# Loading four sets of parameter rows at the start, on ScalarE's queue, in a DeltaNet and attention trunk

## The chip, the cores and the metric

The kernel runs on one core of a Trainium2 chip. The metric is the device time of one execution in microseconds. The median of three runs before the change is 1419.02 us (1417.68 to 1421.04). Less is better.

## The reference, cut to what matters

One sequence of 512 tokens of width 1024 goes through two layers. The first mixes tokens with a gated DeltaNet, the second with sliding-window attention; each ends with a gated MLP that holds a causal depthwise convolution of width 3. All of it is float32.

```
h = x
h = h + gated_deltanet(rmsnorm(h, a_norm_w), a_w_in, a_conv_w, a_a_log, a_dt_bias, a_out_norm_w, a_w_out)
h = h + conv_gated_mlp(rmsnorm(h, ffn_norm_w[0]), ffn_w_up[0], ffn_conv_w[0], ffn_conv_b[0], ffn_w_down[0])
k, v = shared_kv(h, kv_norm_w, w_kv)
h = h + sliding_window_sink_attention(rmsnorm(h, b_norm_w), k, v, b_w_q, b_sinks, b_w_o, bias, mask)
h = h + conv_gated_mlp(rmsnorm(h, ffn_norm_w[1]), ffn_w_up[1], ffn_conv_w[1], ffn_conv_b[1], ffn_w_down[1])
return rmsnorm(h, final_norm_w)
```

The parameters that the change moves are vectors: the taps of the DeltaNet's convolution (a_conv_w, 4 x 4096), those of the MLP's convolutions (ffn_conv_w, 2 x 3 x 5632), the DeltaNet's output norm (a_out_norm_w, 128) and the final norm (final_norm_w, 1024).

## The kernel before, in words

Activations are held with channels on the 128 partitions and the 512 tokens along the free dimension. In that layout a per-channel parameter is wanted as a column: one number for each partition. In memory the parameters are rows. The helper `columns` (lines 227 to 238) makes the one out of the other: it loads up to 128 rows of 128 numbers into a staging tile, one load for each part, turns the tile on TensorE (line 235) into a bank of PSUM, and has VectorE copy it (line 237) into a constant tile. Its arguments choose the queue of the loads (`q`, SP's if nothing is said), the staging buffers (`tag`) and the bank (`place`). PSUM is divided into tags of banks: "d" has 3, "g" 2, "s" 2 and "p" 1. The staging tag "acc" has two buffers, "f" three.

Matmuls run at float32 accuracy as three products of rounded halves (lines 162 to 164): for each weight tile ScalarE makes the high half (line 132, whi) and VectorE the low half (line 133, wlo); activations are split in the same way into xh and xl.

The start runs as follows. SP loads x in four tiles of 128 tokens (line 204) and the first weights (line 210). ScalarE's queue loads the norm rows and MLP biases, and `columns` turns them (norm_c, line 240). For each tile of x, ScalarE sums the squares (line 258) and takes a root (259), and VectorE scales the tile (261). TensorE turns the tiles in eight slabs (line 266), by turns into banks of "s" and "g"; ScalarE and VectorE split each slab while they scale it with a column of norm_c (lines 172 and 173). Then `columns` makes cw_c, the taps of the DeltaNet's convolution (line 273, loaded on SP's queue, bank "g"), which `conv_silu` (lines 275 to 282) reads. The first projection of keys follows, and the gates (lines 305 to 391): two narrow loads on ScalarE's queue (309 and 310), a chain on ScalarE and VectorE, four transposes (370) into a bank of "g", a copy of it by ScalarE (374) and exponentials of it (383 to 391).

Behind the gates stand the other columns: onw_c (17 rows in four loads, line 413) and fcw (128 rows for each of the two MLPs, line 424), all on SP's queue, staged in "f" and turned into banks of "g". The first reader of onw_c is the gating of the DeltaNet's output (line 723), that of fcw the first MLP.

The DeltaNet's heads come in four groups, whose jobs are given a priority by the list ORDER (lines 30 to 38): projections, products of the keys (line 433) and of the decays (464 and 465), the solving of small triangular systems, the scan. A planner at build time puts every engine's instructions in an order, by priority and by when it reckons their inputs to be there; a queue or an engine then runs its own list in that order. SP and ScalarE issue the loads. A load that reuses a completion counter waits for the load that had it before.

Of the kernel before, what the change touches and what calls it, by code (L numbers as in the profile page):

```python
# [17 lines left out]
P = 128  # L18
# [23 lines left out]
def kernel(  # L42
# [27 lines left out]
    V, S, G, PE, SP = nc.vector, nc.scalar, nc.gpsimd, nc.tensor, nc.sync  # L70
# [36 lines left out]
    def row(tag, dt=F32, n=T):  # L107
        return main.tile([P, n], dt, tag=tag, bufs=ROWS[tag], name=nm(tag))
# [4 lines left out]
    def bank(tag):  # L113
        return psum.tile([P, T], F32, tag=tag, bufs=BANKS[tag], name=nm(tag))

    def const(shape, dt=F32, s="c"):
        return cp.tile(list(shape), dt, name=nm(s))
# [109 lines left out]
    def columns(parts, n, s, q=SP, tag="acc", place="g"):  # L227
        st = row(tag, n=P)
        r = 0
        for ap in parts:  # L230
            k = ap.shape[0]
            q.dma_start(st[r : r + k, :], ap)
            r += k
        ps = bank(place)
        PE.transpose(ps[:, :n], st[:n, :], ident[:n, :n])
        t = const([P, n], s=s)
        V.tensor_copy(t[:], ps[:, :n])
        return t
# [11 lines left out]
        q=S,  # L250
    )
    NA, NFFN, NKV, NB, CB = 0, 8, 24, 32, 40


    for c in range(NC):
        junk = main.tile([P, D], F32, tag="nt", bufs=2, name=nm("junk"))
        r = const([P, 1], s="rx")
# [5 lines left out]
    for k in range(KD):  # L263
# [3 lines left out]
        h, l = row("xh", F32R), row("xl", F32R)  # L267
# [2 lines left out]
        xl.append(l)  # L270


    cw_c = columns([a_conv_w[0].rearrange("j (r c) -> (j r) c", c=P)], 128, "cwc")

    def conv_silu(ps, t, o):
        acc = row("acc")
# [99 lines left out]
    def hc(ap):  # L376
# [31 lines left out]
    od = dp.tile([4, P, NC, T], F32, name="od")  # L408
    zd = dp.tile([HV, P, T], F32, name="zd")
    yd = dp.tile([HV, P, T], F32, name="yd")  # L410

    fconv_rows = ffn_conv_w.rearrange("l j (r c) -> l (j r) c", c=P)
    onw_c = columns(
        [
            fconv_rows[0, 128:132, :],
            fconv_rows[1, 128:132, :],
            a_out_norm_w,
            final_norm_w.rearrange("(r c) -> r c", c=P),
        ],
        17,  # L420
        "onwc",
        tag="f",
    )
    fcw = [columns([fconv_rows[l, 0:128, :]], 128, "fcw", tag="f") for l in range(2)]

    def key_norms(g):
        pr = slice(2 * g, 2 * g + 2)
# [1017 lines left out]
```

## Time and profile before

| | |
|---|---|
| median of three runs | 1419.02 us |
| the profiled execution | 1418.66 us |
| its span, first to last instruction | 1416.8 us |
| TensorE busy | 1384.8 us |
| VectorE busy | 1109.1 us |
| ScalarE busy | 748.0 us |
| columns' transposes (line 235) start at | 8.46, 18.99, 42.90, 45.96 (two) us |

All times inside the execution are microseconds from the start of its span. PE is TensorE's matmul side, PEld its weight loads, DVE is VectorE, ACT ScalarE, POOL GpSimd, SP the engine that only issues loads; a "q" behind a name is the engine's queue, in which loads are issued and waited for. A row of a timeline has the start, the duration, engine and line, operation, tile written and tiles read, and in brackets how long the engine had been idle and what ended that.

### The profile page before, as it was taken

To read this page: it belongs to the slowest core of one execution; us is meant where nothing else is said; L and a number is where in the kernel's file an instruction comes from. 1 tells how busy PE (TensorE), PEld (TensorE's weight loads), DVE (VectorE), ACT (ScalarE), POOL (GpSimd) and SP (SyncE) were. 2 spreads that over 40 slices of the span, in tenths; PEclk is the share of its full clock that TensorE was granted. 3 is DMA by queue.
4 is the path that set the end of the run, shared out by engine and by line. 5 is a ranking of instruction groups with operands and counts; after the bars stand their busy time and mean duration, and the time that the engine had idled before them with its cause. 6 is when DMAs were issued, how large, how long until landed. Compare 5 with 4: busy or idle time off the path is not lost.

```text
span 1416.8 us, 21740 instructions
## 1 busy us (share of the span) xinstructions
PE 1384.8 (98%) x8362; PEld 1166.5 (82%) x8362; DVE 1109.1 (78%) x2072; ACT 748.0 (53%) x1470; POOL 15.7 (1%) x37
## 2 busy tenths in 40 slices
PE   7999999999999999999999999999999999999997
PEld 5787888878877888888988889778788888988897
DVE  4996886968856447879878889788658888878996
ACT  7764576656647325444335446567544444444543
POOL 1000000000100000000000000000000000000000
PEclk9999999999999999999999999999999999999999
DMA  5333254172465323221443223322132221432222
GB/s 160 90 104 115 80 174 124 60 230 84 143 221 157 119 86 115 90 90 46 134 149 119 75 73 108 109 76 76 60 112 86 93 90 59 137 107 86 95 75 75
DMA packets 162299, 151.80 MB, mean 107 GB/s; under 512 B 24148, under 2 KB 150677, under 8 KB 162197
## 3 DMA queue, kind: packets, MB, share of 16 engines
q1 hardware_dynamic: 159938, 150.22, 33.0%
q8 instruction: 66, 1.08, 0.3%
q10 hardware_dynamic: 2259, 0.20, 0.1%
q14 instruction: 36, 0.29, 0.1%
HBM read 133.60 MB, written 15.75 MB: 105 GB/s over the span
## 4 chain that ended last, share of the span: by engine, by line
PE 85%; DVE 7%; DMA 4%; ACT 2%; issue 1%; SPq 0%; DVEq 0%; ACTq 0%
PE d L162 20%; PE d L164 20%; PE d L163 20%; PE g L198 2%; DVE wlo L133 2%; PE d L1207 1%; PE d L1211 1%; PE d L1209 1%; PE d L1054 1%; PE d L1052 1%; PE d L1053 1%; PE s L1054 1%; PE p L1303 1%; PE s L659 1%; PE s L1052 1%
## 5 line engine op out<-in xcount | busy, mean ns | idle before, releaser
L162 PE MATMUL d<-xh,whi 128*128 128x512 f32 x1128 | 444.2, 394 | 0.2
L163 PE MATMUL d<-xl,whi 128*128 128x512 f32 x1128 | 444.0, 394 | 0.0
L164 PE MATMUL d<-xh,wlo 128*128 128x512 f32 x1128 | 442.1, 393 | 0.8 <-DVE wlo L133 0.5
L132 ACT CAST whi<-stage 128x1024 fp32r<-128x1024 f32 (+2 forms) x234 | 227.4, 976 | 249.7 <-PE d L163 170.3
L133 DVE TENSOR_TENSOR wlo<-stage,whi 128x1024 fp32r<-128x1024 f32 (+2 forms) x234 | 263.3, 1128 | 70.2 <-ACT whi L132 69.3
L164 PEld LDWEIGHTS d<-xh,wlo 128*128 128x128 f32 x1128 | 211.6, 188 | 45.5 <-DVE wlo L133 1.0
L162 PEld LDWEIGHTS d<-xh,whi 128*128 128x128 f32 x1128 | 211.7, 188 | 44.8 <-ACT xh L172 0.5
L163 PEld LDWEIGHTS d<-xl,whi 128*128 128x128 f32 x1128 | 211.7, 188 | 43.1 <-issue 0.5
L280 DVE SCALAR_TENSOR_TENSOR acc<-d,cwc,acc 128x511 f32<-128x511 f32 (+2 forms) x96 | 70.6, 738 | 8.7 <-ACT acc L277 7.8
L913 DVE TENSOR_TENSOR sz<-d,p6s 128x512 f32<-128x512 f32 x59 | 40.6, 688 | 43.4 <-PE d L164 41.2
L935 ACT ACTIVATE dt<-dt 128x512 f32<-128x512 f32 x44 | 27.8, 632 | 78.3 <-DVE dt L918 78.3
L918 DVE SCALAR_TENSOR_TENSOR dt<-sz,fcw,dt 128x511 f32<-128x511 f32 (+1 forms) x60 | 44.8, 747 | 1.8 <-ACT dt L916 0.9
L918 DVE SCALAR_TENSOR_TENSOR va<-sz,fcw,va 128x511 f32<-128x511 f32 (+1 forms) x58 | 43.3, 747 | 0.9
L561 DVE TENSOR_TENSOR sT<-sT,p6s 64x31 f32<-64x31 f32 (+15 forms) x124 | 40.9, 330 | 2.0
L555 DVE TENSOR_TENSOR p6s<-sN,sT 64x31 f32<-64x31 f32 (+15 forms) x124 | 40.7, 328 | 1.9
L1276 ACT ACTIVATE dt<-dt,sm 128x256 f32<-128x256 f32 (+1 forms) x64 | 30.1, 471 | 21.5 <-DVE sm L1259 21.5
L132 ACT CAST whi<-st 128x768 fp32r<-128x768 f32 (+1 forms) x30 | 23.7, 791 | 30.1 <-PE p L1053 5.8
L913 DVE TENSOR_TENSOR zl<-d,p6s 128x512 f32<-128x512 f32 x29 | 20.0, 688 | 17.8 <-PE d L164 17.8
L682 ACT ACTIVATE rq<-o 128x128 f32<-128x128 f32 x64 | 19.0, 301 | 25.0 <-DVE o L677 22.0
L937 DVE TENSOR_TENSOR va<-dt,va 128x512 f32<-128x512 f32 x44 | 30.4, 690 | 1.2
L133 DVE TENSOR_TENSOR wlo<-st,whi 128x768 fp32r<-128x768 f32 (+1 forms) x30 | 26.8, 899 | 2.2 <-ACT whi L132 2.2
L916 ACT ACTIVATE dt<-sz,normc,fcw 128x512 f32<-128x512 f32 x30 | 24.4, 815 | 6.5 <-DVE sz L913 6.2
(769 smaller groups left out, 2873.2 us busy)
## 6 DMA issues: line engine op xcount, KB each, us to landing
stage<-in_ffn_w_up_dram SPq DMA_DIRECT2D x44, 1024.0 KB, 4.7
stage<-in_a_w_in_dram SPq DMA_DIRECT2D x23, 1024.0 KB, 5.5
stage<-in_ffn_w_down_dram SPq DMA_DIRECT2D x16, 768.0 KB, 4.3
stage<-in_a_w_out_dram SPq DMA_DIRECT2D x8, 1024.0 KB, 5.1
st<-in_ffn_w_down_dram SPq DMA_DIRECT2D x8, 768.0 KB, 5.2
zd<-sz SPq DMA_DIRECT2D x16, 256.0 KB, 2.6
od<-o SPq DMA_DIRECT2D x16, 256.0 KB
stage<-in_b_w_q_dram SPq DMA_DIRECT2D x4, 1024.0 KB, 5.0
```

The costliest lines, as they stand in the source:

```text
L132: S.copy(hi[:, :kt, :m], src)
L133: V.tensor_tensor(lo[:, :kt, :m], src, hi[:, :kt, :m].bitcast(F32), op=ALU.subtract)
L162: PE.matmul(ps, hi[:, k, :m], xh[k], start=first and k == 0, stop=False)
L163: PE.matmul(ps, hi[:, k, :m], xl[k][:], start=False, stop=False)
L164: done.append(PE.matmul(ps, lo[:, k, :m], xh[k], start=False, stop=last and k == kt - 1))
L280: V.scalar_tensor_tensor(acc[:, d:], ps[:, : T - d], col, acc[:, d:], op0=ALU.mult, op1=ALU.add)
L555: V.tensor_tensor(tv, N[:, s, s + 1 : 32].unsqueeze(2).to_broadcast([64, n, m]), Tm[:, s : s + 1, 0:m].to_broadcast([64, n, m]), op=ALU.mult,)
L561: V.tensor_tensor(Tm[:, s + 1 : 32, 0:m], Tm[:, s + 1 : 32, 0:m], tv, op=ALU.subtract)
L913: V.tensor_tensor(u[:], ps[:], rs[:], op=ALU.mult)
L918: V.scalar_tensor_tensor(acc[:, d:], u[:, : T - d], tap(2 - d, t), acc[:, d:], op0=ALU.mult, op1=ALU.add)
L937: V.tensor_tensor(b[:], a[:], b[:], op=ALU.mult)
L1276: S.activation(ej, ej, AF.Exp, bias=ngm[:, i : i + 1], scale=-1.0, accum_out=den[:, i : i + 1])
```

## The change

The three calls of `columns` for cw_c, onw_c and fcw move up, right behind norm_c and ahead of the code that squares, scales and turns x. All their loads go to ScalarE's queue (`q=S`), and each of the four tiles gets a bank: cw_c one of "s", onw_c that of "p", the two of fcw one of "g" and one of "s". What is loaded and computed stays the same.

```
+    cw_c = columns([a_conv_w[0].rearrange("j (r c) -> (j r) c", c=P)], 128, "cwc", q=S, place="s")
+    fconv_rows = ffn_conv_w.rearrange("l j (r c) -> l (j r) c", c=P)
+    onw_c = columns(
+        [
+            fconv_rows[0, 128:132, :],
+            fconv_rows[1, 128:132, :],
+            a_out_norm_w,
+            final_norm_w.rearrange("(r c) -> r c", c=P),
+        ],
+        17,
+        "onwc",
+        q=S,
+        tag="f",
+        place="p",
+    )
+    fcw = [columns([fconv_rows[l, 0:128, :]], 128, "fcw", q=S, tag="f", place="gs"[l]) for l in range(2)]
...
-    cw_c = columns([a_conv_w[0].rearrange("j (r c) -> (j r) c", c=P)], 128, "cwc")
...
-    fconv_rows = ffn_conv_w.rearrange("l j (r c) -> l (j r) c", c=P)
-    onw_c = columns(
...
-        17,
-        "onwc",
-        tag="f",
-    )
-    fcw = [columns([fconv_rows[l, 0:128, :]], 128, "fcw", tag="f") for l in range(2)]
```

More of the change, by code (lines that the diff above doesn't have):

```diff
@@ L410 @@
     yd = dp.tile([HV, P, T], F32, name="yd")
-    fconv_rows = ffn_conv_w.rearrange("l j (r c) -> l (j r) c", c=P)
-    onw_c = columns(
[L414 to L419, printed above, removed]
-        17,
-        "onwc",
-        tag="f",
-    )
-    fcw = [columns([fconv_rows[l, 0:128, :]], 128, "fcw", tag="f") for l in range(2)]
     def key_norms(g):
```

## The prediction

> **What bounds the kernel now.** I read the page first, then the two ends of the stretch that the change touches: TensorE's timeline from 40 us, the waits of the load queues, and the timelines of the first 15 us.
>
> ```profile
> span 1416.8 us, 21740 instructions
> PE 1384.8 (98%) x8362; PEld 1166.5 (82%) x8362; DVE 1109.1 (78%) x2072; ACT 748.0 (53%) x1470; POOL 15.7 (1%) x37
> PE   7999999999999999999999999999999999999997
> ...
> PE 85%; DVE 7%; DMA 4%; ACT 2%; issue 1%; SPq 0%; DVEq 0%; ACTq 0%
> ```
>
> TensorE is busy for 98% of the span and holds 85% of the chain that ended last; only the first and the last of the 40 slices are under 9. So what the change can win is TensorE's idle time, or work taken off it, and what it can lose is a later start of the dense stretch. The whole change plays in the first two slices (35.4 us each). Where the four sets of columns are made now:
>
> ```profile
> 18.76 0.39 PE L164 MATMUL d<-xh,wlo 128*128 128x512 f32 x1
> 18.99 0.27 PE L235 MATMUL g<-ident,acc 128*128 128x128 f32 x1
> ...
> 19.33 0.39 PE L163 MATMUL d<-xl,whi 128*128 128x512 f32 x1
> ```
>
> ```profile
> 42.90 0.23 PE L235 MATMUL g<-ident,f 17*128 17x17 f32 x1
> 43.06 0.50 PE L162 MATMUL d<-xh,whi 128*128 128x512 f32 x1
> 43.39 0.39 PE L163 MATMUL d<-xl,whi 128*128 128x512 f32 x1
> 43.62 0.40 PE L164 MATMUL d<-xh,wlo 128*128 128x512 f32 x1
> 43.86 0.39 PE L162 MATMUL d<-xh,whi 128*128 128x512 f32 x1
> 45.96 0.48 PE L235 MATMUL g<-ident,f 128*128 128x128 f32 x2 [1.72 <-DVE onwc L237]
> 46.20 0.48 PE L163 MATMUL d<-xl,whi 128*128 128x512 f32 x1
> ```
>
> Columns are start, duration, engine and line. A full matmul starts 0.23 us behind the one before it (43.39, 43.62). The transpose of the convolution rows (18.99) sits inside the first projection; that of the 17 mixed rows at 42.90; the two of the channel-mixer's rows at 45.96, after TensorE stood idle for 1.72 us until VectorE's copy of the 17 columns had freed a bank. That is the one hole the change removes. VectorE and ScalarE around it:
>
> ```profile
> 45.09 0.74 DVE L280 SCALAR_TENSOR_TENSOR acc<-d,cwc,acc 128x510 f32<-128x510 f32 x1
> 45.74 0.17 DVE L237 COPY onwc<-g 128x17 f32<-128x17 f32 x1
> ```
>
> ```profile
> 44.17 0.63 ACT L281 ACTIVATE kT<-acc 128x512 f32<-128x512 f32 x1
> 44.71 1.03 ACT L132 CAST whi<-stage 128x1024 fp32r<-128x1024 f32 x1
> 45.64 0.42 ACT L374 COPY gt<-g 128x320 f32<-128x320 f32 x1
> 46.08 1.28 ACT L383 ACT_TABLE_LOAD   x1
> ```
>
> ```profile
> L237 DVE COPY fcw<-g x2: 285/288/290, 46.8 to 47.0; 128x128 f32<-128x128 f32 x2
> ```
>
> ```profile
> 46.00:61.00 15.00, 15.00 (x75) 11.97 (x76) 13.67 (x29) 14.26 (x32) 0.00 (x0) 1.00 0.50 149
> ```
>
> The 0.17 us copy was ready long before; it stood in VectorE's order behind convolution work. The next-to-last row gives the shortest, median and longest of the two copies behind it, in ns. In the last row (busy PE, PEld, DVE, ACT of the 15 us that follow) ScalarE is busy 14.26 of 15.00: behind the hole TensorE isn't far ahead of ScalarE.
>
> **The change, part by part.**
>
> (a) The hole. The transpose at 42.90 goes: the next matmul starts at 42.90 instead of 43.06, 0.16 us. The two at 45.96 go with their wait: the matmul at 46.20 could start at 43.86 + 0.23 = 44.09, 2.11 us. Together 2.27 us, of which 1.72 is idle.
>
> (b) The transpose at 18.99. From 18.76 to the second matmul behind it are 0.57 us instead of 2 x 0.23, so 0.11 us goes.
>
> (c) What is late next. Behind the hole come the products of the keys (line 433) into both banks of "g". They need the keys, ready at 44.17 + 0.63 = 44.80, and their second half the bank that ScalarE's copy of the gates frees at 45.64 + 0.42 = 46.06. With all of (a), the first half would start about 1 us after the matmul at 44.09, some 45.1, last about 0.9 (an estimate from the group of 16 that takes 2.01 in the row below), and meet that bank at 46.0: little is lost there, under 0.1.
>
> ```profile
> 47.21 2.01 PE L433 MATMUL g<-kT 128*128 128x128 f32 x16
> ```
>
> But the 15 us from 46 hold only 0.74 us of ScalarE idleness, and ScalarE makes both the high half of each weight and the operands of TensorE's small products. If TensorE comes 2.27 us early it may wait for ScalarE until 61 us for all but 0.74 us: 1.53 us given back. At the other end nothing is, if the plan fills in projections whose weights are cast already. VectorE gets 0.17 + 0.29 + 0.29 us lighter there, which helps. I take 0.8, the middle: 75 matmuls without a gap in the row above speak for filling, 14.26 us of ScalarE against it.
>
> (d) The front. Loads of both queues share eight completion counters, as these waits show:
>
> ```profile
> SPq L210 <- DMA xt<-in_x_dram: 2.0, 2, 1.0
> SPq L232 <- DMA acc<-in_kv_norm_w_dram: 1.6, 1, 1.6
> SPq L204 <- DMA acc<-in_a_norm_w_dram: 0.9, 1, 0.9
> ```
>
> The fourth load of x (line 204) waited for the landing of one of ScalarE's norm rows, with which it shares no data; so did the convolution rows (line 232) for another's. Three tiles of x and five loads of norm rows stand ahead of that fourth: the ninth load isn't issued before the first has landed, and so on. Now the seven loads come on ScalarE's queue, right behind its five:
>
> ```profile
> 2.51 0.31 ACTq L232 DMA_DIRECT2D acc<-in_ffn_conv_b_dram  x1
> ...
> 4.27 1.06 ACT L258 ACTIVATE junk<-xt 128x1024 f32<-128x1024 f32 x1 [1.39 <-DMA xt<-in_x_dram]
> ...
> 8.16 1.06 ACT L258 ACTIVATE junk<-xt 128x1024 f32<-128x1024 f32 x1 [0.94 <-DMA xt<-in_x_dram]
> ...
> 9.34 0.29 ACT L259 ACTIVATE rx<-rx,eps 128x1 f32<-128x1 f32 x1
> 9.45 0.41 ACTq L309 DMA_DIRECT2D gst<-in_a_w_in_dram  x1
> ...
> 9.73 1.05 ACT L258 ACTIVATE junk<-xt 128x1024 f32<-128x1024 f32 x1
> ...
> 11.11 1.03 ACT L132 CAST whi<-stage 128x1024 fp32r<-128x1024 f32 x1
> 12.89 0.69 ACT L172 ACTIVATE xh<-s,normc 128x512 fp32r<-128x512 f32 x1 [0.75 <-PE s L266]
> ```
>
> Each issue costs 0.31 us of the queue (2.51), and an activation can run beside it (9.45 lies inside 9.34 to 9.63), so the seven issues as such are at nothing: cover is the wait for x, and without it they would cost 7 x 0.31 = 2.2 us. What counts is their order among the squares of x (line 258), which the planner sets. If they are spread among the squares, the last is issued near 9.5 and lands about 3.4 us later by the next row, near 12.9:
>
> ```profile
> gp<-in_a_dt_bias_dram SPq DMA_DIRECT2D x1, 0.1 KB, 3.4
> ```
>
> ```profile
> 8.46 0.45 PE L235 MATMUL g<-ident,acc 128*128 128x128 f32 x1 [8.46 <-DMA xt<-in_x_dram]
> ...
> 10.68 0.47 PE L266 MATMUL s<-ident,xt 128*128 128x128 f32 x1 [0.84 <-DVE xt L261]
> 10.94 0.42 PE L266 MATMUL g<-ident,xt 128*128 128x128 f32 x1
> ...
> 13.63 0.80 PE L162 MATMUL d<-xh,whi 128*128 128x512 f32 x1
> ```
>
> With x's transposes strictly behind, the last parameter transpose ends near 13.2, the four transposes of x's first slab (0.26 us apart, 10.68 to 10.94) near 14.2, and the first xh comes there instead of at 12.89: 1.3 us. If the planner lets x's ready transposes go first, nothing. TensorE itself has the room (idle until 8.46, and 0.84 us before 10.68), VectorE's copies too. I take 0.6, about halfway, since no row is nearer to either end.
>
> A rule bears on this. Why was the gates' load issued only at 9.45?
>
> ```profile
> 1.68 0.42 POOL L307 MEMSET gst<- 128x384 f32 x1
> ```
>
> The tile that it fills had been cleared at 2.10, and the norm rows, one of whose counters it takes over, had all landed when they were transposed at 8.46; still it went only after the activation at 9.34 had begun. So a load stays behind an activation that waits. The Trainium skill ("Perfetto Trace Analysis", section "Sequencer Loop") has the sequencer push an engine instruction into that engine's queue, where it waits, so that a load behind it could go at once; by that the late landing would vanish and (d) would be 0, the sum -1.6 instead of -1.0. The trace speaks against it here, and the sum goes by the trace.
>
> (e) SP's queue loses the same loads; it then issues the two gate parameters and the sinks earlier, for which nothing waited. Its two weight loads may get another counter to wait for; I put that at nothing: the cast of the first weights ended at 11.11 + 1.03 = 12.14, 1.5 us before the first matmul (13.63), and beyond those 1.5 us each microsecond would cost one.
>
> Sum: -2.27 - 0.11 + 0.8 + 0.6 = -1.0 us. The profiled execution took 1418.66 us (span 1416.8 and 1.9 around it), so 1417.7; it lies 0.4 under the median of 1419.02, and on the median the forecast is 1418.0. The forecast's own range: from -1.6 (front free) and -2.4 (all kept) to +0.5 (both bounds bad), 1416.6 to 1419.5. About 2.8 us (0.2%) is what a measurement of this kernel tells from no change; its three runs lie 3.4 us apart.
>
> **The rivals.**
>
> First rival, the whole stall and more is won. If the plan keeps (a) and (b) whole, the front costs nothing, and the new order of the stretch saves ScalarE one table load (1.28 us, the row at 46.08) where it is nearly full, the sum is -2.38 - 1.28 = -3.7: 1415.4. For it: the front has idle TensorE and VectorE, and the stretch from 46 is crowded, so that each microsecond counts. Against: no row says that a table load goes, and one may as well come. With two, -4.9: 1414.1.
>
> Second rival, slower: the loads block ScalarE. If the planner puts all seven ahead of the squares, the last ones wait for a counter that the fourth x tile holds. That tile had landed at 9.73 at the latest (its square), so the first square would start there instead of at 4.27. Squares at 1.06 plus 0.1 (9.22 to 9.34) put the fourth at 9.73 + 3 x 1.16 = 13.2 instead of 9.73, and everything behind it 3.5 us later. If besides (c) gives back 1.53, the sum is -2.38 + 1.53 + 3.5 = +2.7; 1421.7; with the transposes' 1.3 on top +4.0: 1423.0. It decides as soon as the last loads stand ahead of the first square. For it: the loads are ready from the start, and come first in the program. Against: the planner had not put the gates' loads, ready early too, ahead of the squares; they came at 9.45.
>
> Third rival, the change doesn't do what it says: the planner places the new transposes where their banks and data allow, amid x's, and the later stretch is packed anew to the same length: -0.3, 1418.7.
>
> **How the numbers follow.** Forecast 0.42, first rival 0.28, second 0.20, third 0.10. Faster by over 0.2% is the first rival: 0.28. Slower is the second, of which a part stays under 2.8 us: 0.17. Within: 0.55. The range leaves out the far end of the second rival and little of the first: 1414.1 to 1422.4.
>
> **What would show it.** Right: no transposes of line 235 after x's first, the matmuls at 43 to 47 us without a hole, and TensorE at 61 us ahead by 1 to 2 us less what the first xh is late. The first xh later than 14.2, or a ScalarE load standing before the first square with that square later than 5, shows the second rival. TensorE waits on ScalarE between 46 and 61 would show (c) at its bad end. Wrong altogether would be a difference that arises after 75 us, where nothing is touched but the planner's packing.

## The result, and the profile after

| | before | after |
|---|---|---|
| median | 1418.35 us (1415.40 to 1421.04) | 1433.13 us (1432.49 to 1433.46) |
| the profiled execution | 1418.66 us | 1432.97 us |
| its span | 1416.8 us | 1431.2 us |

The ratio is 1.0104 (95% interval 1.0083 to 1.0125): 14.8 us slower, on the side of the second rival and far beyond its price. The page after:

```profile
span 1431.2 us, 21743 instructions
PE 1389.5 (97%) x8362; PEld 1170.3 (82%) x8362; DVE 1106.6 (77%) x2072; ACT 747.8 (52%) x1470; POOL 12.3 (1%) x37
PE   5899999999989999999999999999999999999998
PEclk9999999999989999999999999999999999999999
PE 84%; DVE 7%; DMA 4%; ACT 3%; issue 1%; DVEq 0%; SPq 0%; ACTq 0%
```

TensorE still bounds the kernel. Apart from the last slice, two places differ: the first slices (5, 8 instead of 7, 9), and the twelfth slice (394 to 429 us), where its busy share and, in the row below, its granted clock are at 8.

**The front.** ScalarE, VectorE and TensorE of the kernel after, each as a timeline (start, duration, engine, line, operation, tiles):

```profile
2.85 0.41 ACTq L232 DMA_DIRECT2D acc<-in_a_conv_w_dram  x1
...
8.04 0.85 ACTq L232 DMA_DIRECT2D f<-in_ffn_conv_w_dram  x2
8.93 1.06 ACT L275 ACTIVATE junk<-xt 128x1024 f32<-128x1024 f32 x1 [6.06 <-DMA f<-in_final_norm_w_dram]
...
14.05 1.05 ACT L132 CAST whi<-stage 128x1024 fp32r<-128x1024 f32 x1
```

```profile
10.67 0.15 DVE L277 RECIPROCAL rx<-rx 128x1 f32<-128x1 f32 x1
13.45 0.29 DVE L237 COPY fcw<-g 128x128 f32<-128x128 f32 x1 [2.63 <-PE g L235]
13.66 0.74 DVE L278 TENSOR_SCALAR xt<-xt,rx 128x1024 f32<-128x1024 f32 x1
...
16.31 1.22 DVE L133 TENSOR_TENSOR wlo<-stage,whi 128x1024 fp32r<-128x1024 f32 x1
17.45 0.16 DVE L277 RECIPROCAL rx<-rx 128x1 f32<-128x1 f32 x1
17.64 0.75 DVE L278 TENSOR_SCALAR xt<-xt,rx 128x1024 f32<-128x1024 f32 x1
```

```profile
12.94 0.47 PE L235 MATMUL g<-ident,f 128*128 128x128 f32 x1 [2.40 <-DMA f<-in_ffn_conv_w_dram]
...
14.46 0.47 PE L283 MATMUL s<-ident,xt 128*128 128x128 f32 x1 [0.64 <-DVE xt L278]
...
19.56 0.49 PE L162 MATMUL d<-xh,whi 128*128 128x512 f32 x1 [0.45 <-ACT xh L172]
```

All seven loads stand ahead of the first square, which starts at 8.93 (4.27 before), right behind the end of the last issue (8.04 + 0.85). TensorE then waits for the rows of the parameters in its own order, until 12.94. VectorE had the first tile's factor at 10.67 + 0.15, but its next instruction was the copy of fcw, which waited until 13.45, so the tile was scaled at 13.66. Last, ScalarE casts the first weights at 14.05 (11.11 before), ahead of the last tile's root, and VectorE makes their low half (16.31) ahead of that tile's scaling (17.64). The weights themselves were late too: issued at 7.79 instead of 4.27, they landed 6.2 us later, near 14.0. But the fourth square and its read-out kept ScalarE until 13.95 anyway, so their lateness cost about 0.1 us here; what counts is the order. The first full matmul is at 19.56 instead of 13.63: 5.9 us.

**The old hole.** Around 46 us TensorE still stands idle, for longer, and for another engine:

```profile
47.89 0.50 PE L164 MATMUL d<-xh,wlo 128*128 128x512 f32 x1 [2.75 <-DVE wlo L133]
```

**The tail of the DeltaNet.** In each group VectorE solves the triangular systems; SP stores the result (td, line 566 here) and loads it back in four parts as Xg (line 569); `levels` turns Xg on VectorE (line 578) and builds the full inverses with small matmuls. SP's queue and VectorE's two transposes in the last group:

```profile
392.64 0.58 SPq L566 DMA_DIRECT2D td<-sT  x1
...
394.65 0.55 SPq L122 DMA_DIRECT2D stage<-in_a_w_out_dram  x1
...
399.87 0.65 SPq L569 DMA_DIRECT2D Xg<-td  x1
404.89 0.32 SPq L727 DMA_DIRECT2D yd<-zl  x1
405.26 0.43 SPq L569 DMA_DIRECT2D Xg<-td  x1
...
407.92 0.95 SPq L569 DMA_DIRECT2D Xg<-td  x2
```

```profile
L578 DVE STREAM_TRANSPOSE sy<-Xg x2: 1203/1221/1239, 414.8 to 415.9; 128x1024 f32<-128x1024 f32 x2
```

The same of the kernel before:

```profile
381.48 0.49 SPq L564 DMA_DIRECT2D td<-sT  x1
384.42 0.33 SPq L567 DMA_DIRECT2D Xg<-td  x1
...
392.17 0.42 SPq L567 DMA_DIRECT2D Xg<-td  x1
```

```profile
L576 DVE STREAM_TRANSPOSE sy<-Xg x2: 1203/1224/1245, 395.4 to 396.6; 128x1024 f32<-128x1024 f32 x2
```

From the store to the levels it was 395.4 - 381.48 = 13.9 us; now it is 22.2. Between store and read-back stand a weight load, the loads of the output gates, and a store that waits for VectorE. The last part of the read-back is issued near 408.4, 15.8 us behind the store instead of 10.7, and lands 2.6 us later, near 411.0. The later issue is 5.1 of the 8.3 us. The rest lies in VectorE's order (the changed kernel's timeline):

```profile
410.76 0.75 DVE L725 SCALAR_TENSOR_TENSOR zl<-g,onwc,zl 128x512 f32<-128x512 f32 x1 [1.94 <-DMA zl<-zd]
413.62 1.23 DVE L133 TENSOR_TENSOR wlo<-stage,whi 128x1024 fp32r<-128x1024 f32 x1 [2.11 <-ACT whi L132]
414.76 2.37 DVE L578 STREAM_TRANSPOSE sy<-Xg 128x1024 f32<-128x1024 f32 x2
```

With Xg there since 411.0, VectorE finishes the gating of a head, whose rows came over SP's queue, and then stands before the low half of a weight whose high half ScalarE casts late. TensorE has by then done its full-size matmuls and waits. The busy times by window (us, then PE, PEld, DVE, ACT, POOL, then the granted clock):

```profile
400.00:417.00 17.00, 13.00 (x131) 9.70 (x129) 6.95 (x7) 6.42 (x15) 0.00 (x0) 1.00 0.62 193
417.00:431.00 14.00, 11.01 (x157) 9.44 (x158) 5.56 (x13) 3.91 (x10) 0.61 (x2) 0.51 0.65 218
```

TensorE lacks 4.0 of 17 us, and then runs 14 us at half clock. Before, it was busy for all of the 17 us around its levels.

**An account for all runs.** Shifts of single matmuls mislead where the order differs. So I took the time from the start of each TensorE matmul to the start of the next, less the median of that time for its line and shape over all the traces, and summed what is over: idle time, half clock, small stretches. The parts: when the first full matmul starts; from there to 60 us; from 60 us to 36 us behind the start of the last solve (373.4 before); and the tail from there to the first channel mixer (528.8 before). One execution each; medians and ratios are over all runs. The traced execution is within 1.1 us of its kernel's median except in e7 (1428.29, 5.0 under it), e3 (1421.83, 2.7 under it) and e18 (1422.05, 1.8 above it); there the parts explain the traced execution, not the median.

| kernel | median us | ratio to before (interval) | first full matmul | to 60 us | middle | tail |
|---|---|---|---|---|---|---|
| before | 1418.35 | | 13.6 | 3.1 | 25.5 | 12.8 |
| after | 1433.13 | 1.0104 (1.0083 to 1.0125) | 19.6 | 4.5 | 25.3 | 21.1 |
| e1_sp_queue | 1432.61 | 1.0102 (1.0087 to 1.0117) | 18.1 | 6.1 | 26.1 | 20.3 |
| e2_act_queue_late | 1419.79 | 1.0014 (1.0001 to 1.0027) | 13.3 | 3.8 | 24.0 | 15.4 |
| e3_banks_only | 1424.57 | 1.0042 (1.0027 to 1.0057) | 13.7 | 2.0 | 24.3 | 19.5 |
| e4_conv_only | 1420.83 | 1.0022 (1.0011 to 1.0033) | 13.2 | 3.2 | 26.0 | 16.0 |
| e5_xg_pool | 1432.09 | 1.0095 (1.0076 to 1.0114) | 20.1 | 5.0 | 27.0 | 17.6 |
| e6_filler | 1434.90 | 1.0120 (1.0104 to 1.0136) | 19.3 | 4.5 | 25.3 | 21.1 |
| e7_behind_squares | 1433.32 | 1.0115 (1.0093 to 1.0137) | 18.2 | 2.7 | 24.7 | 20.1 |
| e8_banks_xg_pool | 1423.14 | 1.0034 (1.0023 to 1.0045) | 13.8 | 2.0 | 25.1 | 18.4 |
| e9_after_z4 | 1435.74 | 1.0129 (1.0113 to 1.0145) | 20.4 | 5.0 | 33.1 | 16.1 |
| e10_banks_z4 | 1426.27 | 1.0062 (1.0050 to 1.0075) | 13.6 | 2.0 | 33.4 | 13.6 |
| e11_turn_late | 1435.21 | 1.0128 (1.0109 to 1.0147) | 19.0 | 6.1 | 26.5 | 20.3 |
| e12_before_z4 | 1426.60 | 1.0065 (1.0047 to 1.0083) | 13.8 | 2.3 | 30.7 | 17.4 |
| e13_onw_bank | 1425.66 | 1.0056 (1.0041 to 1.0072) | 13.4 | 2.3 | 24.8 | 21.2 |
| e14_cw_bank | 1418.44 | 1.0001 (0.9988 to 1.0014) | 13.8 | 2.9 | 26.0 | 11.2 |
| e15_hold | 1435.93 | 1.0129 (1.0113 to 1.0145) | 20.1 | 5.8 | 25.8 | 22.0 |
| e16_xg_first | 1429.10 | 1.0080 (1.0065 to 1.0096) | 20.1 | 5.3 | 26.1 | 15.2 |
| e17_banks_xg_first | 1419.90 | 1.0012 (1.0003 to 1.0020) | 13.6 | 4.2 | 25.1 | 15.2 |
| e18_before_xg_first | 1420.27 | 1.0018 (1.0007 to 1.0028) | 13.9 | 4.0 | 26.7 | 14.3 |

After against before: 5.9 at the front, 1.4 to 60 us, nothing in the middle, 8.3 in the tail. That is 15.4. In the traces the first channel mixer starts 14.8 us later (543.62 against 528.79), so the other work comes to about 0.6 less. The two traced executions differ by 14.3 in all, the medians by 14.8.

Order and tail go together. In before, e2, e4 and e14 the levels come 13.9 to 14.3 us behind the store of td, and the tail is 11.2 to 16.0. In after, e1, e3, e7, e11 and e13 they come 21.6 to 22.2 us behind it, and the tail is 19.5 to 21.2, with a late front (after, e1, e7, e11) or without one (e3, e13). Inside each group the tail spreads by some us, so a difference of 1 or 2 us in it says nothing of an edit.

### The profile page after: what moved, and what is told of

Its sections match the earlier page's. It is cut to its first block, busy times and chain, and to the rows that moved or that the text cites. A ratio compares the mean times of both kernels' runs of the same rounds, so it can differ in the third digit from the quotient of the medians.

```text
span 1431.2 us, 21743 instructions
## 1 busy us (share of the span) xinstructions
PE 1389.5 (97%) x8362; PEld 1170.3 (82%) x8362; DVE 1106.6 (77%) x2072; ACT 747.8 (52%) x1470; POOL 12.3 (1%) x37
## 4 chain that ended last, share of the span: by engine, by line
PE 84%; DVE 7%; DMA 4%; ACT 3%; issue 1%; DVEq 0%; SPq 0%; ACTq 0%
PE d L164 19%; PE d L162 19%; PE d L163 19%; PE g L198 2%; DVE wlo L133 2%; PE d L1209 1%; PE d L1213 1%; PE d L1211 1%; PE d L1056 1%; PE d L1054 1%; PE s L653 1%; PE d L1055 1%; PE s L1056 1%; PE p L1305 1%; PE s L1054 1%
## 5 line engine op out<-in xcount | busy, mean ns | idle before, releaser
L296 DVE SCALAR_TENSOR_TENSOR acc<-d,cwc,acc 128x509 f32<-128x509 f32 (+2 forms) x96 | 70.2, 738 | 11.2 <-ACT acc L293 10.5
L920 DVE SCALAR_TENSOR_TENSOR va<-sz,fcw,va 128x511 f32<-128x511 f32 (+1 forms) x58 | 43.4, 748 | 0.9
L684 ACT ACTIVATE rq<-o 128x128 f32<-128x128 f32 x64 | 18.9, 298 | 25.3 <-DVE o L679 18.2
```

What stands on the lines that cost most here:

```text
L296: V.scalar_tensor_tensor(acc[:, d:], ps[:, : T - d], col, acc[:, d:], op0=ALU.mult, op1=ALU.add)
L920: V.scalar_tensor_tensor(acc[:, d:], u[:, : T - d], tap(2 - d, t), acc[:, d:], op0=ALU.mult, op1=ALU.add)
```

## The experiments

My theories after the result were, for the front, that the seven loads on ScalarE's queue block the squares, and for the tail, that the planner's new order of the last group costs the time whatever was moved. The rivals: for the front, TensorE's own order with the parameter transposes ahead of x's; for the tail, a consequence of the late front.

**e1: the loads back on SP's queue.** The changed kernel with, in all three calls,

```
-        q=S,
+        q=SP,
```

> As the changed kernel, but the seven loads stay on SP's queue, behind x and the first weights. Queue theory (ScalarE held by loads ahead of its squares makes the front late): first square at 4.3 us as before, first full matmul at 13.6 to 14.5 instead of 19.56, total about 1428. Order theory (transposes and copies of the rows stand ahead of x's and wait for late rows): the rows now land behind the weights, so the first full matmul stays at 17 or later and the total at 1430 to 1434. Plan theory (most of the later loss hangs on SP's order around the last group's solve): the read-back is split by weight and gating loads, TensorE idles over 2.5 us near 410 and runs at half clock after it, so 1425 or more in either case.

Measured: nothing won. The squares are where they were before, x's tiles are all scaled by 12.1, and still TensorE comes late. VectorE and TensorE:

```profile
11.39 0.75 DVE L277 TENSOR_SCALAR xt<-xt,rx 128x1024 f32<-128x1024 f32 x1
```

```profile
12.54 0.47 PE L235 MATMUL s<-ident,acc 128*128 128x128 f32 x1 [3.28 <-DMA acc<-in_a_conv_w_dram]
13.29 0.26 PE L235 MATMUL p<-ident,f 17*128 17x17 f32 x1 [0.28 <-DMA f<-in_final_norm_w_dram]
14.10 0.47 PE L235 MATMUL g<-ident,f 128*128 128x128 f32 x1 [0.55 <-DMA f<-in_ffn_conv_w_dram]
14.36 0.63 PE L282 MATMUL g<-ident,xt 128*128 128x128 f32 x2
```

x's first transpose (8.70 before) comes at 14.36, behind three that wait for rows in memory; first xh 16.55. VectorE's order is no part of it here: x's tiles were scaled before the copies of the moved columns. So ScalarE's queue isn't all of the front.

**e2: ScalarE's queue alone.** The kernel before, `q=S` in the three calls at their old places.

> As the kernel before, but the seven loads go on ScalarE's queue; the transposes stay where they were. Queue theory in its plain form (loads of rows on ScalarE's queue hold it) would make the front late here too, first full matmul at 15 or later, total 1421 or more. If it is their place ahead of the squares that counts, the front stays: first full matmul at 13.6 within 0.3 and the total 1418 within 2. Plan theory: SP's order around the last solve is that of before, so no late loss.

Measured: first xh 12.6, no loss at the front. One of the seven loads stands between the second and the third square (issued at 6.77), the others are issued from 17.4 on; the queue as such costs nothing there. Its tail has before's order and is 2.6 us longer, with half clock from 407.4 to 414.2 that before hasn't.

**e3: the four banks alone.** The kernel before, with `place` as in the change (s, p, g and s), nothing moved.

> As the kernel before, with the four banks of the change and nothing moved. Plan theory: the front is as before and the hole of 1.7 us at 44 is gone, yet the last group's scan comes late with TensorE idle and at half clock near 410 to 430, and the total is 1418.4 - 2 + 9, about 1425. Rival (the late loss is only the front's delay carried on): without a late front there is no late loss, total 1416 to 1417.

Measured: 0.42% slower, with the front of before. The account to 60 us is 1.1 better, the tail 6.7 worse. So most of the tail's loss needs no move at all. And the hole at 44 us stays, though nothing waits for a bank of columns any more. TensorE and ScalarE:

```profile
44.97 0.71 PE L434 MATMUL g<-kT 128*128 128x128 f32 x4 [1.61 <-ACT gt L374]
```

```profile
43.57 1.03 ACT L132 CAST whi<-stage 128x1024 fp32r<-128x1024 f32 x1
44.50 0.42 ACT L374 COPY gt<-g 128x320 f32<-128x320 f32 x1
```

The products of the keys wait for the bank that ScalarE's copy of the gates frees, and that copy for a cast.

**e4: the convolution's taps alone.** The kernel before with only the call for cw_c moved up (`q=S, place="s"`).

> As the kernel before, with only the taps of the DeltaNet's convolution loaded and turned early, on ScalarE's queue, in a bank of s. Queue theory: one load ahead of the squares waits only for the first norm row (landed at 2.97), but takes its counter, so the fourth tile of x is issued at 4.3 instead of 2.99 and the first full matmul comes 0.5 to 1.3 us late; total 1419 to 1420. Order theory: 0.3 us from the copy at most. Plan theory: no late loss; a total over 1423 would speak against it.

Measured: 0.22% slower; no loss at the front, though this load too stands ahead of the squares: it is issued at 3.16, the first square starts at 4.40, and the rows are there when TensorE turns them at 8.49, ahead of x's first transpose at 8.70. One early load and transpose are hidden. The tail has before's order, with an idle stretch of 2.1 us and half clock for 6.8 us behind it.

**e5 and e8: the read-back on GpSimd's queue.** In the changed kernel (e5) and in e3 (e8):

```
-            SP.dma_start(
+            (G if g == 3 else SP).dma_start(
                 Xg[bs, :, :]...
```

> The changed kernel with one edit: the last group's four loads of the solved blocks (Xg) go on GpSimd's queue, which holds nothing else there, instead of standing behind a weight load and the gating loads on SP's queue. Order theory (the late loss comes from what stands ahead of these loads on SP's queue, and from TensorE's idle time and half clock that follow): the levels come some 8 to 15 us earlier than 414.8, no idle stretch of over 2 us before them, no half clock of 13.7 us, and the time is 1433.1 less the 8.4 us that were lost behind 400 us: 1424 to 1428. Rival (the loads are late only because the solve is; TensorE has nothing else to do there whatever their queue): levels still behind 410 us, 1431 to 1434. The front stays 5 us late under both.

> The kernel before with the four banks alone, nothing moved (1424.6 when measured), and the last group's four loads of Xg on GpSimd's queue. Order theory: the 2.3 us that TensorE was ahead at 350 us are kept, and the loss behind 400 us (6.7 us in the trace) goes: 1414.5 to 1417.5, at or under the kernel before. Rival (whatever takes the hole away is given back late): 1422 to 1425.

Measured: 1.0 us less than the changed kernel (e5) and 1.4 less than e3 (e8), both in the range of the rival. But the test failed in its means: GpSimd's four loads took 12.7 us to issue (e5):

```profile
399.60 0.79 POOL L569 DMA_DIRECT2D Xg<-td  x1 [28.85 <-DMA td<-sT]
...
412.25 0.65 POOL L569 DMA_DIRECT2D Xg<-td  x1 [1.94 <-DMA va<-zd]
```

They landed at 406.55, 409.35, 411.94 and 414.54: each was issued 0.3 us behind the landing of the one before. The levels came at 414.7 as in the changed kernel. Inconclusive for the order.

**e6: filler against the idle stretch.** The changed kernel with 24 transposes that nothing reads:

```
+        if g == 3 and pr == 0:
+            for _ in range(24):
+                behind(PE.transpose(p1[:, 256:384], ident[:], ident[:]), last)
```

> The changed kernel with 24 transposes of the identity, into unused columns of a bank and read by nothing, held behind the last product ahead of the last group's levels, where TensorE stood idle for 2.68 us from 413.5. They compute nothing that is used. Clock theory (the idle stretch itself halves TensorE's clock for 13.7 us, and that costs 5 to 7 us): no half clock behind 415 us, 1426 to 1429. Rival (VectorE's chain of the levels sets the pace there, so that the slow clock costs nothing): 1432 to 1435.

Measured: 1.8 us more than the changed kernel. The 24 transposes ran from 416.07 to 418.91, 0.94 us idle were left ahead of them, and the idle stretch of 2.68 us is gone. Half clock still came, for 3.4 us at 406.6, ahead of the filler, and for 10.2 us at 423.6. The clock theory's number fell: with the levels bare, idle stretches of 0.5 to 0.9 us follow one another there and the clock goes down anyway. The time lies in the rival's range, but with half clock still there the run doesn't show what it costs in this place.

**e7: the loads behind the squares.** The changed kernel, the loads still on ScalarE's queue but behind the fourth square (`behind(d, after)`), the three calls behind the loop that scales x.

> The changed kernel with the seven new loads, still on ScalarE's queue, held behind the fourth square of x, and the three calls of columns behind the loop that scales x. Queue theory for the front (the seven loads ahead of the first square hold ScalarE, and the copies hold VectorE's scaling of x): first square near 4.3, first xh at 13 to 14.5, first full matmul at 13.6 to 15 instead of 19.6; of the 5 us that TensorE was late between 25 and 50 us at most 1 is left, and the late loss stays, so 1427 to 1430. Rival (the new transposes and copies themselves delay x wherever the loads stand): first xh at 16 or later, 1431 to 1434.

Measured: the same median, but the four executions lie 8.3 us apart (1428.29 to 1436.59), and the traced one is the fastest. Squares from 4.15, all tiles scaled by 12.0, yet first xh at 17.10: the transposes stand ahead of x's again, and TensorE waits for their rows until 14.67. The rival held for the front and the median. This trace also shows what half clock costs. It has the same idle stretch as the changed kernel near 46 us (2.74 us, ended by the same wait), but the clock stays up behind it. The changed kernel (first two rows) and e7 (third):

```profile
46.00:54.00 8.00, 6.11 (x27) 5.07 (x28) 6.66 (x12) 4.09 (x7) 0.00 (x0) 0.79 0.50 155
48.60:52.00 3.40, 3.40 (x10) 2.64 (x9) 3.34 (x5) 0.60 (x1) 0.00 (x0) 0.51 0.52 137
```

```profile
46.00:54.00 8.00, 7.83 (x44) 6.59 (x45) 6.97 (x13) 5.38 (x10) 0.00 (x0) 1.00 0.71 232
```

Matmul by matmul the changed kernel is 1.7 us behind e7 before this stretch and 3.3 behind it: 1.6 us for one spell of 3.4 us.

**e11: the transposes behind x's.** The changed kernel with its loads where they are and the four transposes and copies held behind x's last transpose.

> The changed kernel with its seven loads where it has them, on ScalarE's queue ahead of the squares, but with the four transposes and copies held behind the last of x's transposes. What is left of the front's loss is then ScalarE's alone. ScalarE theory (second rival of the prediction): squares still at 8.9 to 13.9, first xh 16 to 16.8 instead of 18.8, first full matmul near 17.3: TensorE 3.2 to 3.8 us late between 25 and 50 us instead of 4.9. Rival (the transposes in TensorE's order are all of it, as in the runs where x's tiles were scaled by 12.1 us and still the first xh came at 16.6 to 17.1): first xh 13 to 14, at most 1 us late. The tail's order is that of the changed kernel, so 1430 to 1433 under the first, 1427 to 1430 under the second.

Measured: first xh at 18.27, later than expected. ScalarE, VectorE and TensorE:

```profile
9.09 1.06 ACT L284 ACTIVATE junk<-xt 128x1024 f32<-128x1024 f32 x1 [6.23 <-DMA f<-in_final_norm_w_dram]
```

```profile
15.62 1.22 DVE L133 TENSOR_TENSOR wlo<-stage,whi 128x1024 fp32r<-128x1024 f32 x1
16.75 0.16 DVE L286 RECIPROCAL rx<-rx 128x1 f32<-128x1 f32 x1
```

```profile
17.75 0.48 PE L292 MATMUL s<-ident,xt 128*128 128x128 f32 x1 [1.84 <-DVE xt L287]
```

By the expectation the blocked squares alone give 16 to 16.8. The rest is the order behind them: ScalarE casts the first weights at 14.02, ahead of the last tile's root (14.96), and VectorE makes their low half ahead of that tile's scaling, behind an instruction that waited 0.8 us for the sinks' load. The weights had landed by 13.5, so it wasn't their lateness. These runs part the two causes of the front. Loads ahead of the squares alone: first xh 18.3. Transposes ahead of x's alone: 16.6 and 17.1. Both: 18.8. Neither (before, e2): 12.9 and 12.6. The two overlap and don't add up.

**e9, e10, e12: the output gates' jobs four places later.** In the changed kernel (e9), e3 (e10) and before (e12):

```
-SHIFT = {"R": 6, "B": -28, "g": -40, "K": -1, "N": 7, "C": -2, "P": -3}
+SHIFT = {"R": 6, "B": -28, "g": -40, "K": -1, "N": 7, "C": -2, "P": -3, "z": 4}
```

> The changed kernel with one number in the planner's table of shifts: the jobs of the output gates (z) come four places later in priority. In this order the last group's loads of Xg stand right behind the store of the solved blocks on SP's queue again, and 33 full-size matmuls stand among the matmuls of the last two levels, where the changed kernel has none and the kernel before 34. Tail theory (the loss behind 390 us is that the levels come late and bare, with TensorE idle and then at half clock, because the gates' projections were spent ahead of them): levels 14 to 16 us behind the end of the solve instead of 23, no half clock of 13.7 us, 1423 to 1427. Rival (the loss is the later end of the solve on VectorE, whatever stands among the levels): 1430 to 1434. The front is the same as in the changed kernel under both.

> The kernel before with the four banks alone (1424.6 when measured) and the same shift of four places for the output gates; here too 33 full-size matmuls stand among the last two levels. Tail theory: the 6.7 us lost behind 390 us go and TensorE's lead of 2.3 us stays: 1414.5 to 1418, the kernel before or a little under it. Rival (the late solve): 1421 to 1425.

> The kernel before with the shift of four places alone, nothing of the change. Control: if the shift were a gain by itself, this would be faster than before. By the tail theory it isn't: in this order 23 full-size matmuls stand among the first of the last two levels and none among the second, between the 34 of before and the none of the changed kernel, and the second Xg load stands behind three others: 1418 to 1423. If the shift itself helps: 1412 to 1416.

Measured: all three totals are worse, above the expected ranges. The account says why: the tails of e9 and e10 are repaired (16.1 and 13.6, no half clock there), but the middle grew from 25.3 and 24.3 to 33.1 and 33.4. My reading, which no run tests, is that the gates' projections fill gaps in the earlier groups too and are missing there when shifted. The theory's place is right, the remedy gives it back.

**e13 and e14: one bank.** The kernel before with one argument each: `place="p"` for onw_c (e13), `place="s"` for cw_c (e14).

> The kernel before with one argument: onw_c is turned in bank p instead of g. Nothing moves, no load changes its queue. In this order no full-size matmul stands among the last two levels, as in the changed kernel. Packing theory (the planner answers a change in the stretch at 42 to 47 us with another order of the last group, and that order costs 6 to 8 us): 1422 to 1426, as with all four banks. Rival (it takes fcw's two banks, or all four): 1416 to 1419.

> The kernel before with one argument: cw_c is turned in bank s instead of g, at its old place and queue. The order of the last group is that of before, with 34 full-size matmuls among the last levels. Packing theory: no loss, 1415 to 1420. Rival (any new bank costs): 1422 to 1426.

Measured: 7.2 us slower (e13) and nothing (e14). The levels of e13, and TensorE's clock behind them:

```profile
L577 DVE STREAM_TRANSPOSE sy<-Xg x2: 1203/1221/1239, 406.6 to 407.7; 128x1024 f32<-128x1024 f32 x2
```

```profile
409.40:423.00 13.60, 11.22 (x158) 9.65 (x159) 5.17 (x12) 4.09 (x10) 0.60 (x2) 0.50 0.64 216
```

Its store of td is issued at 384.4, so its levels come 22.2 us later, as in the changed kernel, with the front of before. The whole tail of the change follows from one argument of an operation of 0.23 us at 43 us.

**e15: full-size matmuls held for the levels.** The changed kernel with 26 matmuls of the last two gate projections held behind steps of the levels.

```
+    HOLD = {14: [(3, 0, 0)], 15: [(0, 0, 1), (3, 0, 2), (5, 1, 1)]}
...
+        for k, pr, step in HOLD.get(h, []):
+            behind(passes[QKV + 128 * h][k], st[3]["step", pr, step])
```

> The changed kernel with 26 full-size matmuls of the last two gate projections held in TensorE's order behind steps of the last two levels; up to some 400 us every order is that of the changed kernel. Filler theory (TensorE lacks full-size matmuls among the levels, so it idles and its clock is halved): 26 x 0.23 = 6 us of work now fill the gaps, no half clock of 13.7 us: 1425 to 1428. Rival (the levels come late and TensorE waits for them in either order; the idle time moves ahead of the levels): 1430 to 1434, with an idle stretch of several us before the first level in place of the small ones.

Measured: 2.8 us more than the changed kernel. The idle time moved ahead of the levels:

```profile
406.27 1.35 PE L198 MATMUL g<-ident,ol 128*128 128x128 f32 x4 [2.82 <-ACT ol L726]
411.11 1.35 PE L198 MATMUL g<-ident,ol 128*128 128x128 f32 x4 [3.25 <-ACT ol L726]
```

The filler theory falls. Work that is saved for the levels is missing ahead of them as long as what TensorE waits for comes late; here that is the output gates' rows, which come over SP's queue too.

**e16, e17, e18: the read-back first on SP's queue.** In the changed kernel (e16), e3 (e17) and before (e18):

```
+            st[g]["solved", b] = SP.dma_start(Xg[bs, ...
...
+        if h >= 9:
+            for d in loads:
+                behind(d, st[3]["solved", 3])
...
+        if m2 == 0:
+            behind(staged[-2], st[3]["solved", 3])
```

> The changed kernel with the output gates' loads of heads 9 and up, and the first weight load of the output projection, held behind the four loads of the solved blocks on SP's queue. Order theory: the first of these loads is issued some 4 us and the last some 8 us behind the store of the solved blocks instead of 7 and 16, the levels come 15 to 18 us behind the solve's end instead of 23, and part of the tail's 8 us is won, less what the later gating loads cost: 1426 to 1430. Rival (VectorE's own order holds the levels): levels 21 us or more behind the solve's end, 1431 to 1436.

> The kernel before with the four banks alone and the loads of the solved blocks held first on SP's queue, as in xg_first. Order theory: the changed kernel won 4.0 us by this; the banks alone (1424.6) win the same: 1419 to 1421.5, levels 7 to 9 us behind the solve's end. Rival (the win was of the front's lateness, which this kernel hasn't): 1423 to 1426.

> The kernel before with the loads of the solved blocks held first on SP's queue, nothing of the change. By the accounts of the traces, TensorE's idle time, half clock and stretched gaps from 36 us behind the last solve's start to the first channel mixer came to 12.8 us in before and 15.2 in the changed kernel with this order. If that order sets the tail, this kernel's tail is some 2 us longer: 1418 to 1421. If earlier levels are a gain by themselves (14.6 us behind the solve's end in before): 1412 to 1416.

Measured: 4.0 us less than the changed kernel (e16), 4.7 less than e3 (e17), 2.1 more than before (e18); e16 and e17 as the order theory expected, e18 as its first case did. SP's queue in e16, and the levels:

```profile
394.18 0.47 SPq L568 DMA_DIRECT2D td<-sT  x1
...
397.44 1.92 SPq L571 DMA_DIRECT2D Xg<-td  x4
```

```profile
L580 DVE STREAM_TRANSPOSE sy<-Xg x2: 1202/1224/1245, 401.2 to 402.4; 128x1024 f32<-128x1024 f32 x2
```

The levels come 7.0 us behind the store instead of 22.2, and the tail's account falls from 21.1 to 15.2. In before the same order is too much: the first weight load of the output projection, issued at 374.7 there, moves to 395.1 in e18, and the time grows by 2.1 (the tail by 1.5, within the spread). That the tail's loss follows the order of the last group is shown from both sides: e13 brings it without a late front, e16 and e17 take most of it away. SP's queue alone isn't separated: in e16 VectorE's order changed with it, and VectorE waits there for nothing but Xg (5.1 us). No version here beats the kernel before.

## Why the prediction was wrong, point by point

Two steps failed. (d) put the front at 0.6 us, 1.3 at most, and it cost 5.9. And the sum has no term for what a new packing does to the rest of the program, which cost 8.3 in the tail. The win of (a) and (c), 1.5, became a loss of 1.4.

- **What bounds the kernel**: right. All of the loss is TensorE's idle time and clock.
- **(a) The hole**: the mechanism failed. Columns' transposes were the last thing waited for, not the only one. With their banks out of the way 1.61 us stay (e3), for the gates' copy, the wait that (c) had put under 0.1. The account to 60 us shows 1.1 won there, not 2.27.
- **(b) The transpose at 18.99**: gone, as said; too small to be seen by itself.
- **(c) What is late next**: said to be under 0.1 for the second bank and 0.8 for ScalarE. In the changed kernel VectorE's low half of the weights came last, 2.75 us, and with the spell of half clock behind it the stretch to 60 us lost 1.4 instead of winning 1.5.
- **(d) The front**: the priced term that failed most. It let x's transposes slip in or follow at 13.2, with a first xh by 14.2; it came at 18.82. Two things were missed: TensorE and VectorE keep their order as strictly as ScalarE, so that transposes and copies that wait for memory hold x's; and the squares were blocked as well. The quoted row of the gates' load behind a waiting activation fits the result, but (d) used it only for loads behind an activation, not for activations behind a load. One reading was wrong as well: the transposes at 10.68 and 10.94 are those of the third tile, into two slabs; x's first ones start at 8.70.
- **(e) SP's weights at nothing**: the reason failed, the price nearly held. They were issued at 7.79 instead of 4.27, beyond the cover of 1.5 us, but by (d)'s failure ScalarE was busy until 13.95 and they landed near 14.0. What counts is that their two halves now stand ahead of the last tile's root and scaling (14.05, 16.31).
- **The second rival**: right in its trigger and in its place (first square at 8.93, priced at 9.73), not in its reason. The loads weren't held by the fourth tile of x: that tile was itself issued only at 5.59, after SP had waited 3.5 us for another tile of x, and landed at 9.96, when all seven loads were out (8.9). Its price at the front, 3.5 us or 4.8 with the transposes' 1.3, was too small: 5.9.
- **Packing**: the point called wrong altogether, a difference that arises behind 75 us, is 8.3 of the 14.8 us. The forecast had no term for it, and gave no reason for leaving it out; the third rival let the later stretch be packed anew, but to the same length. The range was narrow for that reason. One bank argument moved nothing (e14), another 7.2 us (e13).

Why the planner answers an earlier moment at 43 us with that order of SP's queue stays open: only the order and its price were measured.

## What to carry to other kernels

An early load or transpose of a parameter isn't free because its engine has idle time: in an engine's fixed order everything behind it waits for its memory, so put it behind the first work that the main path needs, as in e2, or take so little that its rows are there before that work is (e4). Where a planner packs the whole program, give each edit a term for the new packing, sized by an edit of no content, and look in the new order for loads that the next serial step waits for. To judge such an order, account for idle time and clock stretch by stretch; a repair in one place (e9) can cost as much in another.

## What the runs showed of the hardware

**TensorE's clock.** It went to half behind idle stretches under 3 us: behind 2.75 us (after, 45.1 to 47.9), 2.68 us (after, 413.5 to 416.1) and 1.62 us (e2, 43.4 to 45.0), but not behind 2.74 us in e7 or 1.98 us in before. The spells last 3.4, 6.8, 10.2 or 13.7 us, multiples of 3.4, apart from one that runs into the end of every trace. In each trace they start whole multiples of 3.413 us apart: in after at 48.64 and 417.28, 108 x 3.413. So the phase of an execution decides, with the idle time, whether a stretch is punished. The Trainium skill ("TensorE: Matmul & The Clock Gate", section "What's actually happening") has a free-running window of 3413 ns decide; lengths, starts and chance agree with that here. Its advice in the same page ("Why this matters for your kernels") to avoid gaps over about 3 us doesn't: here shorter ones were enough, and the measurement decides.

**GpSimd's queue** issued four loads one behind the other's landing, 12.7 us from the first to the last (e5), where SP issued the same four in 1.92 us (e16). What holds each of them until the one before has landed stays open.
